# A two-layer decoder trunk: feature tiles that take four weight blocks together instead of two

## The chip, the core and the metric

The kernel runs on one NeuronCore of a Trainium2 chip. The core has five engines, each with an instruction queue of its own, which run side by side: TensorE (PE, matrix products into PSUM; its weight loads are a row of their own, PEld), VectorE (DVE), ScalarE (ACT), GpSimd (POOL) and SyncE (SP, which here issues transfers). The metric is the device time of one execution in microseconds (us). Measurements of this kernel lie close together: three runs gave 2045.58, 2045.59 and 2047.15 us, with a median of 2045.59 us.

## The reference

The computation is a decoder trunk of two layers, 256 tokens of 2048 features, in fp32:

```python
def reference(x, mem, ...):
    for i in range(2):
        if i == 1:
            sk1, sk2, sv = shared_kv(x, kv_norm, w_kv, k_norm, cos, sin)
        u = rms_norm(x, mix_norm[i]) @ w_in[i]
        if i == 0:
            pooled = causal_multiscale_pool(u[..., :1536])          # windows 2, 4, 8, 16
            token_out = einsum('bsgc,gcd->bsgd', pooled, pool_w[0]) * pool_scale[0]
        else:
            o = differential_attention(q1, q2, sk1, sk2, sv, lam)   # 12 heads
            token_out = rms_norm(o, subln_norm[0]) * (1.0 - lam_init)
        mem_out = memory_cross_attention(u[..., 1536:], mem, ...)   # 4 heads
        x = x + concatenate([token_out, mem_out], -1) @ w_out[i]
        x = x + squared_relu_mlp(rms_norm(x, ffn_norm[i]), w_ff1[i], w_ff2[i])
    return x
```

Most of the arithmetic is in the weight matrices: the MLP maps 2048 features to 8192 and back in each layer.

## The kernel before

**Two parts of each number.** A product of fp32 accuracy is made of three fp32r products. Each weight is split into a high part (the value rounded to fp32r, cast by ScalarE, line 157) and a low part (what is left, a subtraction on DVE, line 158). Activations are kept split too: a tile `xs[:, k, :]` has 512 columns, 256 with the high parts of the 256 tokens and 256 with their low parts.

**Tiles of 128 features (`a_part`, the function of the change).** The output tile has 128 features as partitions and the tokens as columns, in one PSUM bank of 512 columns. For each block of 128 × 128 weights there are two matmuls. Line 391 has the high weights as the loaded operand and streams all 512 columns (tokens' high parts into columns 0 to 255, their low parts into 256 to 511); this text calls it the wide matmul. Line 393 has the low weights as the loaded operand and streams the 256 columns of high parts into columns 256 to 511; this is the narrow one. The two halves of the bank are added when it is read. Every matmul loads its weights anew. `a_part` makes the tiles of the pooling features `u`, of both output projections (`wo`), of the MLP's up-projection (`ff`, `x_bank` from `fx`) and of half of its down-projection (`x_bank` and `ff` from `z`).

**The other shapes.** `b_tile` (lines 417 to 419) has activations as the loaded operand and streams 512 weight columns, three matmuls a step. Lines 746 to 748 do the same for the other half of the down-projection, which uses seven products of sums of blocks in place of eight, in "slab jobs" between the `a_part` tiles. `c_tile` (lines 405 to 407) and the pooling map (lines 1020 to 1022) take three matmuls of 256 columns per block: high weights twice, then low weights.

**The ring.** Weights come from memory in the order of use, 512 KB a transfer, issued by SP. `Feed` splits them 512 columns at a time, which is four blocks, a *quad*: one cast and one subtraction for the four. The results go to slots of `hi_ring` and `lo_ring`, six slots each. `feed.block` gives the slices of the next block, and at the first block of a quad it also records the preparation of the quads and slabs ahead (three ahead at most); `feed.used` moves on, and at the fourth block of a quad marks its slot as free for what is recorded later. On the chip a cast waits until the matmuls that read the slot's high part are done, and a subtraction until those that read its low part are. `feed.pos % 4` is the place within the quad.

**The order of the work.** The program records its instructions in the order that the Python text gives, and the framework's scheduler then orders each engine's queue by its own model of priorities and readiness; so the queues are near to the recorded order, but not the same. Small pieces of other work (softmax, conversions) are recorded by `tick()`, which `a_part` calls at the end of each quad. `between`, given only at the end of the down-projection, records slab jobs at places where the block's index is a multiple of four.

The few lines at the ring's end that set which instruction frees what:

```python
        if self.pos % 4 == 0:
            self.fill(job)
        return self.split[job][:2]
```

Of the kernel before, what the change touches and what calls it, by code (L numbers as in the profile page):

```python
# [20 lines left out]
NK = 16  # L21
# [241 lines left out]
def program(ctx, tc, plan, dry, xT, memT, par, lam, cst, wst, yT):  # L263
# [8 lines left out]
    feed = Feed(nc, wst, wp, tp, plan, dry)  # L272
# [10 lines left out]
    def tick():  # L283
        now[0] += 1
        for fn in pend.pop(now[0], []):
            fn()
# [90 lines left out]
    def a_part(ps, w, l, n, ks, xs, first=True, last=True, between=None):  # L377


        ks = list(ks)  # L380
        i = 0
        while i < len(ks):
            if between:
                between(i)
            two = []
            for k in ks[i : i + 2 - feed.pos % 2]:
                two.append((i, k % NK, *feed.block((w, l, k, n, 1))))
                feed.used()
                i += 1
            for c, k, hi, lo in two:  # L390
                nc.tensor.matmul(ps, hi, xs[:, k, :], start=first and c == 0, stop=False)  # L391
            for c, k, hi, lo in two:
                nc.tensor.matmul(  # L393
                    ps[:, T : 2 * T], lo, xs[:, k, 0:T], start=False,
                    stop=last and c == len(ks) - 1,
                )
            if feed.pos % 4 == 0:
                tick()
# [249 lines left out]
    def ffn(l, xs, tags, done):  # L648
# [57 lines left out]
        def up_tile(q, i, ps):  # L706
            a_part(ps, "w_ff1", l, q * NK + i, range(NK), xs)
            if not r:
                r.append(rstd_from("x"))
            y = evict(ps)  # L710

            def first():
                nc.vector.tensor_add(y[:, 0:T], y[:, 0:T], y[:, T : 2 * T])
                stt(y[:, 0:T], y[:, 0:T], 0.0, r[0], ALU.max, ALU.mult)

            at(1, first)
            at(3, lambda: nc.scalar.activation(stage[i % 8], y[:, 0:T], AF.Square))  # L717
            if q == 0 or i > 0:
                convert(i, 3)

        def down_tile(q, n, ps, between=None):
            end = l == 1 and q == 3 and n == 7
            if end:
                c_tile(ps, "w_ff2", l, n, range(q * NK, q * NK + NK), z)
                nc.vector.tensor_add(resid[:, n, :], resid[:, n, :], ps[:, 0:T])
                done(n)
                return
            a_part(ps, "w_ff2", l, n, range(q * NK, q * NK + NK), z, between=between)
            x = evict(ps)

            def add():
                nc.vector.tensor_add(resid[:, n, :], resid[:, n, :], x[:, 0:T])
                nc.vector.tensor_add(resid[:, n, :], resid[:, n, :], x[:, T : 2 * T])
                if q == 3:
                    done(n)

            at(1, add)
# [243 lines left out]
    def group_u(g):  # L981
        up = ups[g % 2]
        for c in range(3):
            ps = mmt("u")
            a_part(ps, "w_in", 0, 3 * g + c, range(NK), xs)
            low = vt("u_c")
            nc.scalar.copy(low, ps[:, T : 2 * T])
            nc.vector.tensor_add(low, ps[:, 0:T], low)
            nc.vector.tensor_mul(up[:, c, 16:], low, x_r[0])
# [387 lines left out]
```

## Time and profile before

| | |
|---|---|
| median of three runs | 2045.59 us |
| the profiled execution: its own time | 2044.93 us |
| the profiled execution: span, first to last instruction | 2043.1 us |
| granted clock of TensorE | 1.000 |
| transfers | 390.75 MB, mean 191 GB/s |
| ScalarE, cast of a quad (L157) | 1193 times, mean 620 ns |
| DVE, subtraction of a quad (L158) | 1193 times, mean 695 ns |

How to read it: one execution is recorded by the hardware profiler. A row of a group gives line, engine, operation, tiles written and read, shapes and the count; then busy time in us, the mean duration of one in ns, and the idle time of the engine before them with what ended most of it. A row of waits gives who waited for whom, the us in total, how many times and the longest. A row in order of time gives the start and the duration in us; neighbours of one kind are merged, with their count behind an x. A row of a stretch gives its two ends, its length, the busy time of engines (PE, PEld, DVE, ACT, POOL as far as they are in it) with the number of instructions, the granted clock, the busy share of the transfers and GB/s. Matmuls are pipelined: the record of one goes on while the next has begun, so durations of matmuls don't add up to time, and the intervals between starts do.

### The profile page before, as it was taken

What the parts mean: (1) busy time and instruction counts of PE and PEld (TensorE: products, weight loads), DVE (VectorE), ACT (ScalarE), POOL (GpSimd) and SP (SyncE); (2) the same over time, 40 slices, a digit from 0 to 9 for tenths busy, and PEclk for the clock granted to TensorE, in tenths of its full rate; (3) what the DMA queues carried; (4) which work ended last, traced back from release to release, by engine and by line L of the source; (5) the groups of instructions that cost most, each with busy time, mean ns of one, the idle gap of its engine ahead of it and who ended that gap; (6) DMA issues with size and microseconds to landing.
All of it is one profiled execution on the core that took longest, in us unless ns stands there. A gap on an engine that the chain in (4) does not pass through costs nothing.

```text
span 2043.1 us, 32257 instructions
## 1 busy us (share of the span) xinstructions
PE 2037.2 (100%) x11060; PEld 1755.3 (86%) x11060; DVE 1716.2 (84%) x3215; ACT 1349.8 (66%) x2505; POOL 51.9 (3%) x67
## 2 busy tenths in 40 slices
PE   9999999999999999999999999999999999999999
PEld 8888888888888888888888888888888888888888
DVE  8888889889879978999766687889879978988997
ACT  7765566666666756768665697566657666666764
POOL 0001200000000000000000000310000000000000
PEclk9999999999999999999999999999999999999999
DMA  9556556555555555655565543656555555565564
GB/s 314 178 181 190 188 174 206 197 196 197 186 201 202 189 207 191 207 169 182 194 228 186 170 140 103 196 166 207 196 196 205 186 196 196 186 210 195 196 209 135
DMA packets 110470, 390.75 MB, mean 191 GB/s; under 512 B 12256, under 2 KB 14944, under 8 KB 110304
## 3 DMA queue, kind: packets, MB, share of 16 engines
q1 hardware_dynamic: 110160, 388.59, 57.1%
q8 instruction: 86, 1.41, 0.3%
q14 instruction: 80, 0.66, 0.1%
q10 hardware_dynamic: 144, 0.10, 0.0%
HBM read 386.54 MB, written 2.10 MB: 190 GB/s over the span
## 4 chain that ended last, share of the span: by engine, by line
PE 99%; ACT 1%; DVE 1%; issue 0%
PE x_bank L391 33%; PE x_bank L393 16%; PE wo L391 6%; PE p L746 5%; PE p L747 5%; PE p L748 5%; PE wo L393 3%; PE u L391 2%; PE ff L391 2%; PE u L393 1%; PE k L417 1%; PE k L419 1%; PE v L417 1%; PE k L418 1%; PE v L419 1%; PE v L418 1%
## 5 line engine op out<-in xcount | busy, mean ns | idle before, releaser
L157 ACT CAST hi_ring<-raw 128x512 fp32r<-128x512 f32 x1193 | 736.7, 620 | 529.5 <-PE x_bank L391 308.0
L158 DVE TENSOR_TENSOR lo_ring<-raw,hi_ring 128x512 fp32r<-128x512 f32 x1193 | 817.2, 695 | 206.7 <-ACT hi_ring L157 165.5
L391 PE MATMUL x_bank<-fx,hi_ring 128*128 128x512 f32 x1920 | 602.1, 395 | 0.0
L393 PEld LDWEIGHTS x_bank<-fx,lo_ring 128*128 128x128 f32 x1920 | 361.0, 188 | 83.6
L393 PE MATMUL x_bank<-fx,lo_ring 128*128 128x256 f32 x1920 | 377.4, 278 | 0.0
L391 PEld LDWEIGHTS x_bank<-fx,hi_ring 128*128 128x128 f32 x1920 | 301.4, 189 | 9.3
L391 PE MATMUL x_bank<-z,hi_ring 128*128 128x512 f32 x960 | 301.1, 395 | 0.0
L158 DVE TENSOR_TENSOR lo_ring<-slab,hi_ring 128x1024 fp32r<-128x1024 f32 x188 | 230.1, 1224 | 54.3 <-ACT hi_ring L157 53.6
L157 ACT CAST hi_ring<-slab 128x1024 fp32r<-128x1024 f32 x188 | 196.9, 1047 | 73.1 <-PE x_bank L391 36.2
L393 PEld LDWEIGHTS x_bank<-z,lo_ring 128*128 128x128 f32 x960 | 180.5, 188 | 41.7
L393 PE MATMUL x_bank<-z,lo_ring 128*128 128x256 f32 x960 | 188.8, 278 | 0.0
L391 PE MATMUL wo<-cat,hi_ring 128*128 128x512 f32 x512 | 162.5, 398 | 0.5 <-DVE resid L639 0.5
L391 PEld LDWEIGHTS x_bank<-z,hi_ring 128*128 128x128 f32 x960 | 151.9, 189 | 6.5 <-ACT room L672 0.4
L393 PEld LDWEIGHTS wo<-cat,lo_ring 128*128 128x128 f32 x512 | 95.9, 188 | 21.7
L672 ACT COPY room<-x_bank 128x512 f32<-128x512 f32 x180 | 104.9, 583 | 2.0 <-PE x_bank L393 2.0
L393 PE MATMUL wo<-cat,lo_ring 128*128 128x256 f32 x512 | 101.4, 279 | 0.0
L746 PE MATMUL p<-hi_ring,sit 128*128 128x512 f32 x256 | 100.5, 393 | 0.0
L747 PE MATMUL p<-hi_ring,sit 128*128 128x512 f32 x256 | 100.2, 391 | 0.0
L748 PE MATMUL p<-lo_ring,sit 128*128 128x512 f32 x256 | 99.7, 389 | 0.0
L391 PEld LDWEIGHTS wo<-cat,hi_ring 128*128 128x128 f32 x512 | 79.1, 189 | 2.2 <-PE wo L393 0.9
L717 ACT ACTIVATE room<-room 128x256 f32<-128x256 f32 x128 | 53.2, 416 | 39.1 <-DVE room L300 39.1
L746 PE MATMUL p<-hi_ring,z 128*128 128x512 f32 x192 | 75.2, 392 | 0.0
(313 smaller groups left out, 3102.3 us busy)
## 6 DMA issues: line engine op xcount, KB each, us to landing
raw<-in_w SPq DMA_DIRECT2D x595, 512.0 KB, 4.0
slab<-in_w SPq DMA_DIRECT2D x124, 512.0 KB, 3.3
resid<-in_x SPq DMA_DIRECT2D x8, 256.0 KB, 5.9
room<-in_w SPq DMA_DIRECT2D x4, 512.0 KB, 4.2
memraw<-in_mem SPq DMA_DIRECT2D x4, 512.0 KB, 3.6
out_y<-resid SPq DMA_DIRECT2D x16, 128.0 KB, 1.8
memraw<-in_mem SPq DMA_DIRECT2D x7, 256.0 KB, 6.3
raw<-in_w SPq DMA_DIRECT2D x3, 256.0 KB, 3.5
```

The costliest lines, as they stand in the source:

```text
L157: self.nc.scalar.copy(hi, src)
L158: self.nc.vector.tensor_sub(lo, src, hi.bitcast(F32))
L391: nc.tensor.matmul(ps, hi, xs[:, k, :], start=first and c == 0, stop=False)
L393: nc.tensor.matmul(ps[:, T : 2 * T], lo, xs[:, k, 0:T], start=False, stop=last and c == len(ks) - 1,)
L417: nc.tensor.matmul(ps[t], xl, hi, start=k == 0, stop=False)
L418: nc.tensor.matmul(ps[t], xh, hi, start=False, stop=False)
L419: nc.tensor.matmul(ps[t], xh, lo, start=False, stop=k == NK - 1)
L672: nc.scalar.copy(x, ps)
L717: at(3, lambda: nc.scalar.activation(stage[i % 8], y[:, 0:T], AF.Square))
L746: nc.tensor.matmul(ps, a[1], hi, start=first, stop=False)
L747: nc.tensor.matmul(ps, a[0], hi, start=False, stop=False)
L748: nc.tensor.matmul(ps, a[0], lo, start=False, stop=last)
```

## The change

`a_part` walks the blocks of a quad together. Before, a step took two blocks (one, where the place in the quad is odd), with their wide matmuls first and then their narrow ones. Now it takes all blocks that are left of the quad, four as a rule, so that four wide matmuls stand ahead of four narrow ones. Nothing else is edited.

```diff
-            two = []
-            for k in ks[i : i + 2 - feed.pos % 2]:
-                two.append((i, k % NK, *feed.block((w, l, k, n, 1))))
+            some = []
+            for k in ks[i : i + 4 - feed.pos % 4]:
+                some.append((i, k % NK, *feed.block((w, l, k, n, 1))))
                 feed.used()
                 i += 1
-            for c, k, hi, lo in two:
+            for c, k, hi, lo in some:
                 nc.tensor.matmul(ps, hi, xs[:, k, :], start=first and c == 0, stop=False)
-            for c, k, hi, lo in two:
+            for c, k, hi, lo in some:
                 nc.tensor.matmul(
                     ps[:, T : 2 * T], lo, xs[:, k, 0:T], start=False,
                     stop=last and c == len(ks) - 1,
                 )
```

## The prediction

> **What bounds the kernel now.** I read first, on the page, the busy shares and the chain that ended last, then who waited for whom, then the order of time on TensorE.
>
> ```profile
> span 2043.1 us, 32257 instructions
> PE 2037.2 (100%) x11060; PEld 1755.3 (86%) x11060; DVE 1716.2 (84%) x3215; ACT 1349.8 (66%) x2505; POOL 51.9 (3%) x67
> PE 99%; ACT 1%; DVE 1%; issue 0%
> ACT hi_ring L157 <- PE x_bank L391: 347.4, 499, 2.0
> PEld mk L419 <- DVE lo_ring L158: 0.2, 1, 0.2
> ```
>
> TensorE is never out of work: 99% of the chain is its own. The two rows of waits say who follows whom. ScalarE, which casts the high parts, stood 347.4 us until L391 gave a ring slot back; the weight side of TensorE waited for the ring once, 0.2 us. The casts run ahead of TensorE, so the time is the sum of the intervals from one matmul's start to the next. A matmul's own duration doesn't give these, because the records overlap:
>
> ```profile
> L391 PE MATMUL x_bank<-fx,hi_ring 128*128 128x512 f32 x1920 | 602.1, 395 | 0.0
> L393 PE MATMUL x_bank<-fx,lo_ring 128*128 128x256 f32 x1920 | 377.4, 278 | 0.0
> L391 PE MATMUL x_bank<-z,hi_ring 128*128 128x512 f32 x960 | 301.1, 395 | 0.0
> L391 PE MATMUL wo<-cat,hi_ring 128*128 128x512 f32 x512 | 162.5, 398 | 0.5 <-DVE resid L639 0.5
> L391 PE MATMUL u<-xs,hi_ring x192: 389/396/581, 75.0 to 157.5; 128*128 128x512 f32 x192
> L391 PE MATMUL ff<-fx,hi_ring x128: 393/396/583, 254.2 to 1372.1; 128*128 128x512 f32 x128
> L391 PE MATMUL ff<-z,hi_ring x48: 393/396/479, 931.1 to 2031.8; 128*128 128x512 f32 x48
> ```
>
> (The last three are from the view of line L391: least, median and greatest duration.) The change touches 1920 + 960 + 512 + 192 + 128 + 48 = 3760 blocks, each with one wide matmul (512 columns, L391) and one narrow one (256, L393): 940 quads, walked today as wide, wide, narrow, narrow, twice over.
>
> An interval is read from a long stretch: its first row, its last, and the count between, which the view of stretches confirms (its x is the number of matmuls).
>
> ```profile
> 186.67 0.63 PE L391 MATMUL wo<-cat,hi_ring 128*128 128x512 f32 x2
> ...
> 253.55 0.63 PE L391 MATMUL wo<-cat,hi_ring 128*128 128x512 f32 x2
> 186.67:253.54 66.87, 60.35 (x192) 29.23 (x193) 1.00 0.62 192
> 1025.17 0.39 PE L418 MATMUL v<-hi_ring,x_kv 128*128 128x512 f32 x1
> ...
> 1109.06 0.39 PE L419 MATMUL mv<-lo_ring,mems 128*128 128x512 f32 x1
> ```
> 1025.17:1109.05 83.88, 83.88 (x371) 1.00 0.64 213
> 158.00 0.28 PE L1020 MATMUL pw<-pooled,hi_ring 128*128 128x256 f32 x1
> ...
> 161.12 0.28 PE L1022 MATMUL pw<-pooled,lo_ring 128*128 128x256 f32 x1
> 158.00:161.11 3.11, 3.11 (x26) 3.11 (x27) 0.13 (x1) 0.81 (x2) 1.00 0.67 219
> ```
>
> - Mixed, in the output projection: 192 wide matmuls are 96 pairs of blocks, so a turn (wide, wide, narrow, narrow) takes (253.55 − 186.67) / 96 = 696.7 ns.
> - Wide only, in the value projection: 371 matmuls of which the first began ahead of the stretch, so 370 intervals: (1109.06 − 1025.17) / 370 = 226.7 ns each.
> - Narrow only, in the pooling map: (161.12 − 158.00) / 26 = 120.0 ns each, the granted clock (1.00) being the same in all three.
>
> Two of each at their steady intervals make 2 × 226.7 + 2 × 120.0 = 693.4 ns. A turn takes 3.3 ns more. That excess is all that the order of the blocks can be blamed for, and it is small: 1880 turns × 3.3 = 6.2 us of 2043.1. Where it sits shows on one turn:
>
> ```profile
> 300.06 0.39 PE L391 MATMUL x_bank<-fx,hi_ring 128*128 128x512 f32 x1
> 300.29 0.28 PE L393 MATMUL x_bank<-fx,lo_ring 128*128 128x256 f32 x1
> ...
> 300.40 0.28 PE L393 MATMUL x_bank<-fx,lo_ring 128*128 128x256 f32 x1
> 300.52 0.40 PE L391 MATMUL x_bank<-fx,hi_ring 128*128 128x512 f32 x1
> ...
> 300.76 0.40 PE L391 MATMUL x_bank<-fx,hi_ring 128*128 128x512 f32 x1
> ```
>
> The first narrow one takes 0.11 us (under 120 ns), the second 0.12, the next wide one 0.24 (over 226.7). Each turn wins a little on the way from wide to narrow and loses somewhat more on the way back.
>
> **The change part by part.** The regrouping leaves each matmul, its weight load and its operands as they are: 3760 wide and 3760 narrow, no more and no fewer instructions on any engine. A quad is now four wide and then four narrow. In the built order of the two programs the ways from L391 to L393 fall from 1879 to 949 (920 quads stand as four and four; the rest are cut by other matmuls or by quads that straddle a tile's end).
>
> *The turns.* If the excess belongs to the turn, it falls with their number: 930 × 3.3 ns = 3.1 us are removed. Bounds: none of it, if it belongs to the block and not to the turn (gain 0); all of it, if a run of four leaves each kind time to settle (gain 6.2 us). I take one cost per turn, since the excess is seen at the turn in the rows above and the long runs of one kind have none; 3.1 us.
>
> *When the narrow run begins.* L393 of a quad's first block now starts after four wide ones, not two, so DVE has 2 × 0.23 us longer for the low part. All four low parts are one subtraction, so nothing later is needed earlier. The high slot is given back after the fourth wide matmul, which now has four narrow ones behind it in place of two: 2 × 0.12 us earlier for the cast, which is the 347.4 us waiter above. The low slot is given back at the same place. With 0.2 us of waiting for the ring in all, neither can be seen in the time: 0. The cover is the casts' head start; without it each late cast would cost up to one cast, 620 ns:
>
> ```profile
> L157 ACT CAST hi_ring<-raw 128x512 fp32r<-128x512 f32 x1193 | 736.7, 620 | 529.5 <-PE x_bank L391 308.0
> 277.00:920.00 643.00, 643.00 (x3494) 554.50 (x3493) 563.34 (x976) 429.58 (x731) 0.00 (x0) 1.00 0.58 196
> ```
>
> *What the scheduler moves.* On SP and POOL nothing moves, so every transfer is issued where it was. On ScalarE and DVE neighbours swap places, mostly a cast of the next quad ahead of the copy that makes z's high half (L676), and some of the splits of x_kv and x_mx at the end of layer 0. The first are covered by ScalarE's idle time: in the stretch 277 to 920 us, the first layer's MLP, the last row shows it busy 429.58 of 643 us and DVE 563.34. One L746 in each layer, which stood alone ahead of two quads, joins its L747: same count, 0. Of the last matmuls nothing changes (a tile of three narrow matmuls per block, not this function). Swaps late in layer 0 could delay a split by one cast, 0.6 us, once or twice; I take 0 and keep 1 us for the range.
>
> *The sum.* The profiled execution took 2044.93 us (span 2043.1 and 1.8 around it), 0.7 below the median of the runs, 2045.59. Profile: 2044.93 − 3.1 = 2041.8. Against the median: 2045.59 − 3.1 = 2042.5 us.
>
> **The rivals.**
>
> *The excess goes whole* (2039.4 us = 2045.59 − 6.2). For it: in the wide stretch and the narrow one no excess is left after many of a kind. Against it: one way to and one way back stay in each quad, and the rows show that these cost.
>
> *Narrow matmuls keep the short interval.* In the turn above two took 300.52 − 300.29 = 0.23 us, 115 ns each. If all four in a row do, and the wide ones settle at 226.7, a quad takes 4 × (226.7 + 115) = 1366.8 ns in place of 2 × 696.7 = 1393.4: 940 × 26.6 = 25 us, 2020.6. Against it: the 26 narrow ones settle at 120.0.
>
> *Nothing happens* (2045.6). The excess belongs to blocks: each wide weight block and each narrow one pays alike wherever it stands, as when each load had to be waited for. The Trainium skill, TensorE: Matmul & The Clock Gate, section "The mechanism" of the part on packing small matmuls, says that weight loads overlap running matmuls only when the row group differs. All loads here fill the whole array, so by that rule the order could not matter and the time would stay. The trace disagrees with the rule itself: the load for the second narrow matmul starts as the first one does.
>
> ```profile
> 300.29 0.19 PEld L393 LDWEIGHTS x_bank<-fx,lo_ring 128*128 128x128 f32 x1
> L393 PEld LDWEIGHTS x_bank<-fx,lo_ring 128*128 128x128 f32 x1920 | 361.0, 188 | 83.6
> ```
>
> *Slower: loads run dry in the narrow run.* Such a load lasts 188 ns in the mean, longer than a narrow interval. If the head start that loads win under wide matmuls lasts for two narrow ones only, the third and fourth each wait for a whole load: 2 × (188 − 120) = 136 ns a quad, 940 quads, 128 us: 2045.6 − 3.1 + 127.8 = 2170. It cancels the gain from 3.1 us / 1880 = 1.6 ns for each of these matmuls, and is slower by over 0.2% from 3.8 ns. Against it: in the pooling stretch 27 loads go under 26 matmuls at 120.0. But there two of three in a row load the same high block, so four fresh blocks in a row are shown nowhere; small prices of this kind are the likeliest way to a slower kernel.
>
> *Slower: a starved ring.* If swapped casts come late at each of some 65 places on ScalarE, 65 × 0.62 = 40 us: 2086. The 0.2 us of waiting speaks against it.
>
> **How the numbers follow.** A measurement of this kernel tells 0.2%, 4.1 us, from no change: faster is below 2041.5, slower above 2049.7. The forecast, 2042.5 with its own range of 2040.5 to 2044.5, has 0.45; the whole excess 0.23; short narrow intervals 0.06; nothing 0.13; loads run dry 0.09, mostly at a few ns; a starved ring 0.04. Faster: 0.23 + 0.06 + 0.04 of the forecast's lower edge = 0.33. Slower: the last two, 0.13. Within: 0.41 + 0.13 = 0.54. The range takes in the whole excess with 2 us below it for narrow matmuls a little short, and no change with the 1 us for late splits: 2037.4 to 2046.6. It leaves out the short intervals and the slower two, 0.19.
>
> **What would show it.** The counts per line stay. In the output projection a quad takes about 1390 ns in place of 1393; in a run of four, the second and third narrow matmuls start 0.12 us apart and the third and fourth wide ones 0.23. Waits of TensorE for the ring stay under 1 us, and ScalarE's wait for L391 stays the longest. I am wrong if narrow intervals within a run differ from 120 by more than 4 ns, if a turn now costs twice what it did, or if TensorE waits for L157 or L158.

## The result and the profile after

The changed kernel takes 2057.66 us in the median of six runs (2057.24 to 2058.52), beside 2045.59 us for the kernel before on the same chip (six runs). The ratio is 1.0059 with a 95% interval of 1.0049 to 1.0070: 12 us slower, where 3 us less were forecast, and outside the range. The profiled executions' spans differ by 12.8 us, 2055.9 against 2043.1.

First the lines of the page of the changed kernel that answer to those shown of before (busy shares; chain that ended last; costliest groups):

```profile
span 2055.9 us, 32264 instructions
PE 2049.2 (100%) x11060; PEld 1762.2 (86%) x11060; DVE 1718.9 (84%) x3215; ACT 1349.5 (66%) x2505; POOL 51.9 (3%) x67
PE 99%; ACT 1%; DMA 0%; DVE 0%; SPq 0%; issue 0%
L391 PE MATMUL x_bank<-fx,hi_ring 128*128 128x512 f32 x1920 | 522.4, 393 | 0.0
L393 PE MATMUL x_bank<-fx,lo_ring 128*128 128x256 f32 x1920 | 304.8, 281 | 0.0
```

And from its views of waits, of all engines and of the weight loads:

```profile
ACT hi_ring L157 <- PE x_bank L391: 336.3, 475, 1.9
PEld mk L417 <- ACT hi_ring L157: 0.6, 1, 0.6
PEld mk L419 <- DVE lo_ring L158: 0.4, 1, 0.4
```

The same instructions are there, TensorE is still the whole chain, ScalarE still waits for TensorE by hundreds of us, and TensorE's two waits for the ring, both in the first stage (mk, the memory's keys), make 1.0 us in all. So hardly anything new is waited for: the intervals between matmuls themselves have grown. Fallen busy times of the two groups say nothing about that; matmuls of one group now overlap more with their own kind.

The same stretch of the output projection, in the changed kernel's order of time and view of stretches:

```profile
186.94 1.09 PE L391 MATMUL wo<-cat,hi_ring 128*128 128x512 f32 x4
...
254.30 1.09 PE L391 MATMUL wo<-cat,hi_ring 128*128 128x512 f32 x4
186.94:254.29 67.35, 52.41 (x192) 32.80 (x193) 1.00 0.59 189
```

192 wide matmuls are 48 quads: (254.30 − 186.94) / 48 = 1403.3 ns a quad, where before it was 2 × 696.7 = 1393.4, and at the steady intervals it would be 1386.8. The four and four were to save some 3 ns and cost 10.

A tile of the MLP and the products behind it:

```profile
301.63 1.08 PE L391 MATMUL x_bank<-fx,hi_ring 128*128 128x512 f32 x4
302.55 0.64 PE L393 MATMUL x_bank<-fx,lo_ring 128*128 128x256 f32 x4
303.02 1.09 PE L391 MATMUL x_bank<-fx,hi_ring 128*128 128x512 f32 x4
303.95 0.63 PE L393 MATMUL x_bank<-fx,lo_ring 128*128 128x256 f32 x4
304.42 1.09 PE L391 MATMUL x_bank<-fx,hi_ring 128*128 128x512 f32 x4
...
307.23 0.40 PE L746 MATMUL p<-hi_ring,sit 128*128 128x512 f32 x1
...
309.31 1.07 PE L391 MATMUL x_bank<-fx,hi_ring 128*128 128x512 f32 x4
```

The first quad, behind products, takes 303.02 − 301.63 = 1.39 us, the second 1.40. In both, four narrow matmuls take 0.47 us, 118 ns each, just under the steady 120. But the second quad's four wide ones take 303.95 − 303.02 = 0.93 us, 232 ns each: the longer run of wide ones hasn't brought them to 226.7. And the nine products behind the tile, wide matmuls of another line that the diff doesn't touch, take 309.31 − 307.23 = 2.08 us, 231 ns each.

Summed over the trace, from each matmul's start to the next one's, the wide ones of `a_part` went from 877.8 to 874.7 us, its narrow ones from 436.1 to 446.2, the products from 306.8 to 312.0, and all else from 417.8 to 418.4: −3.1 + 10.1 + 5.2 + 0.6 = 12.8 us, the whole difference of the spans. (These intervals, and the means below, are counted from the starts of all matmuls in the traces.)

### The profile page after: what moved, and what is told of

Read it like the earlier page. It is cut to its first block, busy times and chain, and to the rows that moved or that the text cites. A ratio compares the mean times of both kernels' runs of the same rounds, so it can differ in the third digit from the quotient of the medians.

```text
span 2055.9 us, 32264 instructions
## 1 busy us (share of the span) xinstructions
PE 2049.2 (100%) x11060; PEld 1762.2 (86%) x11060; DVE 1718.9 (84%) x3215; ACT 1349.5 (66%) x2505; POOL 51.9 (3%) x67
## 4 chain that ended last, share of the span: by engine, by line
PE 99%; ACT 1%; DMA 0%; DVE 0%; SPq 0%; issue 0%
PE x_bank L391 32%; PE x_bank L393 17%; PE wo L391 6%; PE p L748 5%; PE p L747 5%; PE p L746 5%; PE wo L393 3%; PE u L391 2%; PE ff L391 2%; PE u L393 1%; PE k L417 1%; PE k L419 1%; PE k L418 1%; PE v L417 1%; PE v L419 1%; PE v L418 1%
## 5 line engine op out<-in xcount | busy, mean ns | idle before, releaser
L391 PE MATMUL x_bank<-fx,hi_ring 128*128 128x512 f32 x1920 | 522.4, 393 | 0.0
L391 PEld LDWEIGHTS x_bank<-fx,hi_ring 128*128 128x128 f32 x1920 | 336.7, 189 | 53.4
L393 PEld LDWEIGHTS x_bank<-fx,lo_ring 128*128 128x128 f32 x1920 | 294.1, 188 | 40.4
L393 PE MATMUL x_bank<-fx,lo_ring 128*128 128x256 f32 x1920 | 304.8, 281 | 0.0
L391 PE MATMUL x_bank<-z,hi_ring 128*128 128x512 f32 x960 | 260.9, 393 | 0.0
L393 PEld LDWEIGHTS x_bank<-z,lo_ring 128*128 128x128 f32 x960 | 147.0, 188 | 20.1
L393 PE MATMUL x_bank<-z,lo_ring 128*128 128x256 f32 x960 | 152.4, 281 | 0.0
L391 PE MATMUL wo<-cat,hi_ring 128*128 128x512 f32 x512 | 141.8, 397 | 0.3 <-DVE resid L639 0.2
L393 PE MATMUL wo<-cat,lo_ring 128*128 128x256 f32 x512 | 82.7, 281 | 0.0
L748 PE MATMUL p<-lo_ring,z 128*128 128x512 f32 x192 | 76.1, 397 | 0.0
```

Of the source, the lines that this page charges most:

```text
L393: nc.tensor.matmul(ps[:, T : 2 * T], lo, xs[:, k, 0:T], start=False, stop=last and c == len(ks) - 1,)
L748: nc.tensor.matmul(ps, a[0], lo, start=False, stop=last)
```

## The experiments

Two views stand against each other: that something of the wide-and-narrow order itself costs (and then what of it), or that the loss comes with the order, from the queues or from what the narrow matmuls touch. Each edit is to the changed kernel's `a_part`.

### Four together, but emitted two and two

The walk is written out as a text, H for the wide matmul of a block and L for its narrow one:

```diff
+            walk = "H0H1L0L1H2H3L2L3" if len(some) == 4 else "".join(
...
+            for kind, j in zip(walk[::2], walk[1::2]):
+                c, k, hi, lo = some[int(j)]
...
```

> The four blocks of a quad are taken together as in the changed kernel, but the matmuls go out as two wide, two narrow, two wide, two narrow. If the length of the narrow run sets the cost (theory), the time is that of the kernel before, 2045.6 us within 1, and a wide matmul after a pair of narrow ones is back at 227 ns from the third on. If the loss comes from taking four blocks at once, through the order that the scheduler then gives to ScalarE and DVE (rival), it stays near 2057.

2045.69 us, ratio 1.0002 (0.9992 to 1.0011). Taking four blocks at a time costs nothing by itself. About the queues this run says nothing: with the old order of the matmuls the scheduler also gave ScalarE and DVE their old order back. Compared place by place with the kernel before, 6 of their 5720 instructions differ here, and 476 in the changed kernel. Three and one, below, settles that.

### One and one; three, two, one, two

Here the text of the walk is edited, against the run above:

```diff
-            walk = "H0H1L0L1H2H3L2L3" if len(some) == 4 else "".join(
+            walk = "H0L0H1L1H2L2H3L3" if len(some) == 4 else "".join(
```

> One wide, one narrow, all through a quad. If what counts is the length of the narrow run (theory), a turn gets cheaper still, under the 3.3 ns of a run of two; at a fifth of the cost per narrow matmul the whole takes 2039 to 2045 us. If every turn has a cost of its own whatever the run (the prediction's view), twice as many turns cost 6 us more: about 2052.

2059.64 us, ratio 1.0065 (1.0048 to 1.0082): slower than four and four. So the length of the narrow run alone doesn't set the cost, and neither view had the size. Cut into pieces of six turns, the unbroken stretches of the trace make 465 pieces of 2106.2 ns in the mean: 351.0 a turn, 4.3 ns over the steady 226.7 + 120.0, a little more than the 3.3 of a turn of two, and there are twice as many. The mean hides two cases. In 140 pieces six turns take 2079 to 2085 ns, which is the steady intervals' 6 × 346.7 or little more, and in 317 they take 2105 to 2121, up to 6.8 ns a turn over. So one and one can run without a loss; what decides it stays open.

```diff
-            walk = "H0H1L0L1H2H3L2L3" if len(some) == 4 else "".join(
+            walk = "H0H1H2L0L1H3L2L3" if len(some) == 4 else "".join(
```

> Three wide, two narrow, one wide, two narrow. Narrow runs stay at two, wide runs become three and one (five across quads do not occur). If the narrow run alone sets the cost: about 2045.6 us. If the lag left by narrow matmuls is paid off under the wide ones that follow, one wide matmul is too few after two narrow ones, and some of it is carried into the next run: 2047 to 2052 us.

2051.41 us, ratio 1.0029 (1.0018 to 1.0040). No narrow run is longer than two, the number of turns is that of before, and 6 us are lost. In its order of time (its line 395 is the wide matmul, 397 the narrow one):

```profile
302.63 0.87 PE L395 MATMUL x_bank<-fx,hi_ring 128*128 128x512 f32 x3
303.33 0.40 PE L397 MATMUL x_bank<-fx,lo_ring 128*128 128x256 f32 x2
303.57 0.39 PE L395 MATMUL x_bank<-fx,hi_ring 128*128 128x512 f32 x1
303.80 0.40 PE L397 MATMUL x_bank<-fx,lo_ring 128*128 128x256 f32 x2
304.03 0.85 PE L395 MATMUL x_bank<-fx,hi_ring 128*128 128x512 f32 x3
```

The quad takes 304.03 − 302.63 = 1.40 us, as in the changed kernel. This fits the second reading: the lag that narrow matmuls leave is carried on when the wide run behind them is short.

The run also answers for the queues. Of the 5720 instructions of ScalarE and DVE, 14 stand elsewhere than before. So the order of the matmuls makes a loss with practically the old order on those engines.

### Narrow matmuls in the other half of the bank

```diff
-                    ps[:, T : 2 * T], lo, xs[:, k, 0:T], start=False,
+                    ps[:, 0:T], lo, xs[:, k, 0:T], start=False,
```

> As the changed kernel, but the narrow matmuls add into columns 0 to 255 of the bank in place of 256 to 511 (the two halves are added later in any case). If the lag comes from narrow matmuls adding into columns that the wide one before wrote last (rival), the wide matmuls return to 227 ns and the time falls by 5 us or more, to 2052 or less. If it comes from the run of short matmuls and their loads (theory), nothing changes: 2057.7 within 1 us.

2057.92 us, ratio 1.0059 (1.0044 to 1.0074), and the same intervals. Which half of the bank the narrow matmuls write has no part in it.

### Eight and eight; three, three, two

These and the last two groupings cross quads, so the slots of a quad are given back after the group that uses it. `sizes` is 8, 8 or 3, 3, 2, 3, 3, 2 in a tile of 16 blocks that begins at a quad; elsewhere groups of two stay:

```diff
-            for k in ks[i : i + 4 - feed.pos % 4]:
+            for k in ks[i : i + (sizes.pop(0) if sizes else 2 - feed.pos % 2)]:
                 some.append((i, k % NK, *feed.block((w, l, k, n, 1))))
-                feed.used()
+                feed.used(hold=True)
                 i += 1
...
+            feed.release()
```

> Eight wide, then eight narrow, where a tile of 16 blocks begins at a quad (slots are given back after the group). If each narrow matmul in a row adds to the lag that the wide ones pay (one theory), a turn costs far more than in the changed kernel and the time is above 2062 us. If the lag stops growing (about 37 ns after four narrow ones, paid off within ten wide ones), a turn of eight costs at most that, with half as many turns: 2052 to 2059 us.

2048.41 us, ratio 1.0013 (1.0004 to 1.0023), below both ranges: not only does the lag stop growing, it is paid off sooner than I had it. The order of time of this kernel (its line 399 is the wide matmul, 401 the narrow one):

```profile
300.74 1.98 PE L399 MATMUL x_bank<-fx,hi_ring 128*128 128x512 f32 x8
302.55 1.12 PE L401 MATMUL x_bank<-fx,lo_ring 128*128 128x256 f32 x8
303.51 2.00 PE L399 MATMUL x_bank<-fx,hi_ring 128*128 128x512 f32 x8
305.35 1.11 PE L401 MATMUL x_bank<-fx,lo_ring 128*128 128x256 f32 x8
306.30 0.40 PE L755 MATMUL p<-hi_ring,sit 128*128 128x512 f32 x1
```

Eight wide ones behind products take 302.55 − 300.74 = 1.81 us, which is 8 × 226.7; behind narrow ones 305.35 − 303.51 = 1.84. Averaged over the 239 turns of the trace that follow eight narrow matmuls, the wide intervals are 233.3, 235.8, 228.3, 232.5, 230.8, and then 226.7: a lag of 27 ns, paid over five matmuls. The first narrow ones have 113.3 and 119.2, the rest 120.0: 7 ns are won on the way from wide to narrow. A whole turn costs 20 ns, more than any other, but there are few.

> Groups of three, three, two, three, three, two blocks in a tile of 16. If the cost rises with the length of the narrow run (theory), three lies between two and four: 2047 to 2055 us. If the cost of a turn depends on how the intervals of a pattern fit together, as one and one (2059.6) and two and two (2045.6) suggest, nothing orders three between its neighbours, and the time can lie outside, below 2045 or above 2057.

2049.62 us, ratio 1.0019 (1.0010 to 1.0029). It lies between two and four, as the first view says, but this can't tell the views apart.

### Narrow matmuls of 320 and of 192 columns

```diff
-                    ps[:, T : 2 * T], lo, xs[:, k, 0:T], start=False,
+                    ps[:, T - 64 : 2 * T], lo, xs[:, k, 0 : T + 64], start=False,
```

> The changed kernel with narrow matmuls of 320 columns; the 64 added columns add products that don't belong there. 64 columns more cost 26.7 ns in each of 3760, 100 us in all: 2158 us if nothing else changes. If the lag arises because a narrow matmul is as short as the load under it, it is gone here: wide ones at 227 ns from the second on, 12 us less, 2143 to 2147 us. If it arises from any change of length (rival), wide matmuls stay at 230 to 236 after the narrow run.

2155.32 us in one run, 2.7 below what the columns alone would give and far above the case without a lag. In the order of time:

```profile
321.13 1.09 PE L391 MATMUL x_bank<-fx,hi_ring 128*128 128x512 f32 x4
322.06 0.74 PE L393 MATMUL x_bank<-fx,lo_ring 128*128 128x320 f32 x4
322.64 0.39 PE L746 MATMUL p<-hi_ring,sit 128*128 128x512 f32 x1
```

Four wide ones still take 0.93 us, 232 ns each, behind narrow ones of 0.145 us. So 64 columns more don't take the lag away. But by the record a weight load lasts 188 ns, still longer than this narrow matmul, so the load isn't excluded as the cause; nothing was run in which narrow matmuls start more than 188 ns apart.

```diff
-                    ps[:, T : 2 * T], lo, xs[:, k, 0:T], start=False,
+                    ps[:, T : 2 * T - 64], lo, xs[:, k, 0 : T - 64], start=False,
```

> The changed kernel with narrow matmuls of 192 columns, which leaves out a quarter of the low products. If a narrow run is bound by its streamed columns, its intervals shrink by 26.7 ns to 93, and the time falls by 100 us to 1958. If it is bound by the weight loads, which take 120 ns each in a row, the intervals stay at 120 and the time at 2050 or above.

2088.43 us in one run, above 2050, but the time can't be used: a tile is now so short that TensorE waits for its one PSUM bank to be read out (view of waits, weight loads):

```profile
PEld x_bank L391 <- ACT room L672: 62.2, 60, 2.0
```

The intervals can be. In the order of time of the output projection:

```profile
201.39 1.10 PE L391 MATMUL wo<-cat,hi_ring 128*128 128x512 f32 x4
202.33 0.58 PE L393 MATMUL wo<-cat,lo_ring 128*128 128x192 f32 x4
202.76 0.41 PE L391 MATMUL wo<-cat,hi_ring 128*128 128x512 f32 x1
```

Four take 202.76 − 202.33 = 0.43 us: in the mean of 506 quads with quads on both sides 86.3, 113.2, 113.3 and 111.5 ns. The third doesn't follow the second in the 93 ns that the columns would allow (an estimate from the two steady intervals), so something else sets the pace here, at 113 ns. The weight loads, which in this stretch also start 113 ns apart, are the likely bound; no run shows it alone. The narrow matmuls of 256 columns, at 120, are above that pace. The wide matmul behind the four takes 252 ns.

### Six, two; fourteen, two

By now the intervals gave a rule. Behind three or more steady narrow matmuls wide ones lose 27 ns over five; but where only two wide ones stand there, the two narrow ones behind them come 11.7 ns early, and the next wide ones lose 10 ns and are in step. A long group and a group of two together should cost what two groups of two cost, however long the long one is.

> Groups of six, two, six, two blocks in a tile of 16 (elsewhere two). Theory, from the intervals of the runs so far: after three or more narrow matmuls in step the wide ones lose 6.7, 9.2, 1.7, 5.8, 4.2 ns and are then back in step (27.5 ns); when two wide ones of these are followed by two narrow ones, the narrow ones win back 11.7 ns and the next wide ones lose only 10 ns and are in step again. So a long group and a group of two together cost 6.7 ns, as two groups of two do. Half as many such pairs in some 420 places of eight blocks: 2.8 us less than before, 2042.0 to 2043.5 us. If cost goes by the length of the narrow run (rival), six are worse than four for each turn: 2050 us or more.

2043.05 us, ratio 0.9986 (0.9977 to 0.9995), as the theory has it. The intervals do too: in the mean of 241 places the two wide matmuls behind six narrow ones take 233.4 and 235.8 ns, the two narrow ones then 115.8 and 112.6, and the next wide ones 232.5, 230.9 and then 226.7.

> Groups of fourteen and two blocks in a tile of 16 (elsewhere two). By the same theory one pair of turns of 6.7 ns in 16 blocks in place of four: 211 tiles x 20 ns = 4.2 us less than before, 2041 to 2042.5 us, if the four slots that a group holds don't starve TensorE. If they do, waits of TensorE for the ring casts (L157, L158 of the kernel before) appear and the time is above 2045 us.

2041.40 us, ratio 0.9979 (0.9970 to 0.9988): the fastest of all, 4.2 us less than before by the medians. In its order of time:

```profile
300.14 3.34 PE L399 MATMUL x_bank<-fx,hi_ring 128*128 128x512 f32 x14
303.31 1.84 PE L401 MATMUL x_bank<-fx,lo_ring 128*128 128x256 f32 x14
304.98 0.63 PE L399 MATMUL x_bank<-fx,hi_ring 128*128 128x512 f32 x2
305.45 0.39 PE L401 MATMUL x_bank<-fx,lo_ring 128*128 128x256 f32 x2
305.68 0.40 PE L755 MATMUL p<-hi_ring,sit 128*128 128x512 f32 x1
```

A tile takes 305.68 − 300.14 = 5.54 us; in the changed kernel it is 307.23 − 301.63 = 5.60. Fourteen wide ones take 226 ns each, fourteen narrow ones 119, and the two and two behind them 0.47 and 0.23 us. Its longest wait of a weight load for the ring is in the first stage (mk), where no tile of this kind runs:

```profile
PEld mk L426 <- ACT hi_ring L158: 1.0, 1, 1.0
```

Four slots held at once don't starve TensorE. And of the 5720 instructions of ScalarE and DVE, 1383 stand elsewhere than before, more than in any other of these groupings, in the fastest of them: the queues are not what costs.

| order of a tile's 16 blocks | median, us | ratio to before |
|---|---|---|
| 1, 1, ... | 2059.64 | 1.0065 |
| 4, 4, 4, 4 (the change) | 2057.66 | 1.0059 |
| 3, 1, 3, 1 wide with 2 narrow each | 2051.41 | 1.0029 |
| 3, 3, 2, 3, 3, 2 | 2049.62 | 1.0019 |
| 8, 8 | 2048.41 | 1.0013 |
| 2, 2, ... (as before, from a group of four) | 2045.69 | 1.0002 |
| 6, 2, 6, 2 | 2043.05 | 0.9986 |
| 14, 2 | 2041.40 | 0.9979 |

Eight, eight and fourteen, two have the same number of turns and lie 7 us apart: what the short second group does to the lag is worth more than the number of turns.

## Why the prediction was wrong, step by step

- *TensorE's intervals are the time*: right. They account for all of the 12.8 us.
- *No other engine matters; the ring, ScalarE's and DVE's queues at 0*: right, by the waits, by three and one, which loses 6 us with the queues of before, and by fourteen and two.
- *The number of turns falls from 1879 to 949*: right.
- *"I take one cost per turn, since the excess is seen at the turn in the rows above and the long runs of one kind have none"*: this step failed. A turn costs 3.3 ns at two and two, and 1403.3 − 1386.8 = 16.5 ns at four and four. 949 × 16.5 = 15.7 us in place of 1880 × 3.3 = 6.2 makes 9.5 us of the loss; the lag that a tile hands to the products behind it makes 5.2 more, and quads that begin behind products, in step or nearly, give some back. Neither bound of this term, none removed or all of it, let a turn cost more than it did.

The error lies in the excess of 3.3 ns itself. The prediction saw a gain and a loss at the turn, but scaled only what was left of the two. It is the difference of two large terms that the same trace shows: leaving out intervals over 262 ns, where other work stands between, a wide matmul of before takes 232.6 ns, 5.9 over its steady 226.7, and a narrow one 115.4, 4.6 under its steady 120.0. Over 3760 blocks this is a loss of 22 us and a gain of 17. The gain comes at the first narrow ones of each run, so it falls with the number of turns: after the change it is 120.0 − 118.4 = 1.6 ns, 6 us in all. The loss on the wide ones I expected to shrink with the turns too. It fell only to 231.5 − 226.7 = 4.8 ns, 18 us, because four wide matmuls are too few to get into step. Behind eight narrow ones, with wide ones in step before them, that takes five, as eight and eight shows. Where the lag is carried on from quad to quad it takes nine: behind the last quad of the changed kernel's tile, nine products in a row take 235.0, 233.4, 235.8, 224.2, 230.8, 235.8, 228.4, 232.5 and 230.8 ns (means of 56 places), and only the wide matmuls behind them 226.7.

The rows at hand could have warned. In the turn that I quoted, the wide matmuls of 0.24 us are the rule and not the exception, and the wide stretch and the narrow one that gave the steady intervals had no turn in them, so they could not tell how long a turn is felt.

Of the rivals, the slower ones named the wrong places. *Loads run dry* fell: the third and fourth narrow matmuls of a quad take 119 ns, not 188. *A starved ring* fell. *The excess goes whole*, *short narrow intervals* and *nothing happens* fell with the sign. The forecast's own sign of error, "if a turn now costs twice what it did", is what came, five times and not twice.

## What to carry to other kernels

A mean excess over steady intervals is not a cost that can be shared out by counting: split it by kind first, since a gain on one kind and a loss on the other can nearly cancel and then scale differently. Where matmuls of two lengths alternate on a full TensorE, try several groupings and read the start-to-start intervals, since the time is not ordered by the length of the groups: here a short group behind a long one beat both the shortest and the even ones.

## What the hardware showed unexpectedly

Matmuls in fp32r, each with a load of its own, run at 226.7 ns (512 columns) and 120.0 ns (256) in step, and a change of length is felt by up to nine matmuls behind it, also by those of another line, PSUM bank and loaded operand. In eight and eight each place of a turn repeats within 0.5 ns (standard deviation) over 239 turns; other groupings have patterns that run over several turns, and one and one has two. The Trainium skill, TensorE: Matmul & The Clock Gate, section "Back-to-back issue gap", gives one spacing for each number of columns, in a stream of loads and matmuls as for an isolated matmul, and doesn't speak of the matmuls before. The traces disagree: a wide matmul here takes 224 to 236 ns by what stood before it. Which part of TensorE keeps this memory was not settled. The half of the bank that is written is excluded as its cause, the weight load isn't, and the place in memory of what narrow matmuls stream was not varied.
